# Seven GpSimd operations in the first up step, and two output weight tiles in other places, in a one-core decoder layer

## The chip, the core and the metric

The kernel runs on one core of a Trainium2 chip. The metric is the device time of one execution in microseconds (us). PE is TensorE, DVE is VectorE, ACT is ScalarE, POOL is GpSimd, and SP issues the transfers of this kernel.

## What is computed

One decoder layer on x (1024 rows of 1024, float32). The part that the change touches is the end of the output projection and the start of the MLP:

```python
mixed = concat(out_a, out_b)            # two attention head groups
x  = x + einsum('bse,ed->bsd', mixed, w_out)
hn = rmsnorm(x, mlp_norm_g)
hid = square(relu(einsum('bsd,df->bsf', hn, w_up)))     # 1024 -> 4096
x  = x + einsum('bsf,fd->bsd', hid, w_down)
```

## The kernel before

Every large product is made of float32r parts: `split` (L74 to L80) writes the high part of a tensor with a cast (ACT, L77) and the low part with a subtraction (L80, on POOL or DVE). Three products then stand for one: high by high, high by low, low by high. `mm` is L73, so every matmul of the kernel has that line.

**Output projection.** For each of eight row tiles dt of the transposed output, `out_weights(dt, e0)` loads a weight block `wor` (two buffers), and splits it into a tile `wos`: high part by ACT, low part by POOL. It is called 16 times, counted by i. Calls 1 to 8 are the first halves of the sum (`out_first`, run beside the attention units of the last heads; the partial sums go to `part_d`, after ACT copies them as `pc` and POOL adds them to `xt`). Calls 9 and 10 are the second halves of dt = 0 and 4, run beside the last attention units. Calls 11 to 16 are those of dt = 1, 5, 2, 6, 3, 7, behind the units: 24 products each, which are for each of four inputs e four with the high part of the weights and then two with their low part. The tile of call i lies in the place `w0` or `w1`, by `i % 2`, so a cast of call 11 has to wait until PE has done with call 9.

**Between the two.** `out_finish` (L938 to L959) loads the partial sum as h, adds PE's bank (DVE, L940), writes h to `h_d`, and makes the inputs of the MLP: for each of seven Strassen-like combinations n a high part `bh` (ACT) and a low part `bl` (DVE, L930 or L80), of which some are of sums `ts` (DVE, L947, L959). Nearly all of that is DVE's work, in one order.

**Up.** `up(j)` for j = 0 to 15 takes a raw block `wur` (`up_load`, two transfers, L982), makes four sums `wus` of its quarters with DVE (`plus` L1002, `minus` L999), and splits seven weights n = 1, 2, 3, 6, 7, 5, 4 into tiles `wu`: ACT casts, and the low part is DVE's for n = 2, 6, 5 and POOL's for the others. The places of the `wu` tiles rotate over `w0` to `w6`: the first two of j = 0 lie in `w5` and `w6`. The h of dt = 0 to 3 lie in `w2`, those of dt = 4 to 6 in `w3`, so the `wu` tiles there wait until h has been written out.

**What sets the order.** Each engine runs one instruction stream in order. The framework's scheduler fixes the streams when the program is built; a stream doesn't change when something is late on the chip. Down (L1080 and after) follows up and isn't touched.

Of the kernel before, what the change touches and what calls it, by code (L numbers as in the profile page):

```python
# [9 lines left out]
F32R = mybir.dt.float32r  # L10
# [6 lines left out]
P = 128  # L17
# [38 lines left out]
def hybrid_layer(  # L56
# [13 lines left out]
    nc = tc.nc  # L70

    def mm(out, lhsT, rhs, start, stop):
        return nc.tensor.matmul(out, lhsT, rhs, start=start, stop=stop)  # L73

    def split(hi, lo, src, hi_eng, lo_eng):
        if hi_eng is nc.scalar:
            hi_eng.copy(hi, src)  # L77
        else:
            hi_eng.tensor_copy(hi, src)
        lo_eng.tensor_tensor(out=lo, in0=src, in1=hi.bitcast(F32), op=ALU.subtract)  # L80
# [123 lines left out]
    for t in LAST:  # L204
        eng = (nc.vector.tensor_copy, nc.scalar.copy)[t % 2]
# [604 lines left out]
    def slot(tag, name, shape, dt=F32, pool="zl"):  # L810
        return o[pool].tile([P] + shape, dt, tag=tag, name=name, bufs=1)
# [26 lines left out]
    def out_weights(dt, e0):  # L838
        i = nout[0] = nout[0] + 1
        wr = o["zl"].tile([P, 4, P], F32, tag="wor", name="wor", bufs=2)  # L840
        nc.sync.dma_start(wr, w_o[dt][:, e0 : e0 + 4, :])
        w = slot(f"w{i % 2}", "wos", [2, 4, P], F32R)
        split(w[:, 0], w[:, 1], wr, nc.scalar, nc.gpsimd)
        return w[:, 0], w[:, 1]

# [15 lines left out]
    def out_first(dt):  # L861
        xt = slot(f"w{2 + dt % 2}", "xt", [S])
        nc.sync.dma_start(xt, xT[dt * P : (dt + 1) * P, :])
        w = out_weights(dt, 0)
        ps = first_banks()
        with paced():
            out_products(ps, w, range(4))
        t = slot("w4", "pc", [S])
        for c in range(2):
            cs = slice(c * 512, (c + 1) * 512)  # L870
            nc.scalar.copy(t[:, cs], ps[c])
            nc.gpsimd.tensor_tensor(out=xt[:, cs], in0=xt[:, cs], in1=t[:, cs], op=ALU.add)
        nc.sync.dma_start(part_d[dt], xt)
# [15 lines left out]
    for dt in (0, 4):  # L889
        ps = first_banks() if dt == 0 else [  # L890
            pa.tile([P, 512], F32, tag="sc", name=f"po{c}", bufs=2) for c in range(2)
        ]
        ahead_of.append((dt, ps, out_weights(dt, 4)))
# [85 lines left out]
    def up_load(j):  # L979
        raws[j] = slot(f"r{j % 2}", "wur", [2, KT, P])  # L980
        for i in range(2):
            up_loads[j] = nc.sync.dma_start(raws[j][:, i], w_u[j + i * NJ])  # L982

    for dt in (1, 5, 2, 6, 3, 7):
        w = out_weights(dt, 4)
        ps = [bank(f"po{c}") for c in range(2)]
        out_products(ps, w, range(4, 8))
        out_finish(dt, ps)
        if dt in (2, 3):
            with tc.issue_after(part["load"].ins):  # L990
                up_load(dt - 2)
# [6 lines left out]
    def minus(out, a, b, eng=nc.vector):  # L998
        eng.tensor_tensor(out=out, in0=a, in1=b, op=ALU.subtract)  # L999

    def plus(out, a, b, eng=nc.vector):
        eng.tensor_tensor(out=out, in0=a, in1=b, op=ALU.add)  # L1002
# [3 lines left out]
    def w_slot(name, shape, dt=F32):  # L1006
        nw[0] = (nw[0] + 1) % NW
        return slot(f"w{nw[0]}", name, shape, dt)
# [3 lines left out]
    def up(j):  # L1012
        if 0 < j < NJ - 1:
            up_load(j + 1)
        raw = raws.pop(j)
        s = slot(*(("m4", "wus", [4, 4, P]), ("m5", "wus", [4, 4, P], F32, "zr"))[j % 2 == 0])
        a11, a12, a21, a22 = raw[:, 0, :4], raw[:, 0, 4:], raw[:, 1, :4], raw[:, 1, 4:]
        plus(s[:, 0], a21, a22)
        minus(s[:, 1], s[:, 0], a11)
        minus(s[:, 2], a11, a21)  # L1020
        minus(s[:, 3], a12, s[:, 1])
        src = {1: a11, 2: a12, 3: s[:, 3], 4: a22, 5: s[:, 0], 6: s[:, 1], 7: s[:, 2]}
        m = {}
        for n in UP:
            w = w_slot("wu", [2, 4, P], F32R)
            split(w[:, 0], w[:, 1], src[n], nc.scalar, nc.vector if n in (2, 6, 5) else nc.gpsimd)
            m[n] = bank(f"pu{n}")
            for k in range(4):
                mm(m[n], w[:, 0, k], bh[n][:, k], k == 0, False)
                mm(m[n], w[:, 0, k], bl[n][:, k], False, False)  # L1030
                mm(m[n], w[:, 1, k], bh[n][:, k], False, k == 3)
            if n == 2 and j == 0:
                part.pop("rest")()
            if n == 1:
                u = slot("m1", "u", [4, 512])
                b = slot("m2", "hb", [4, 512])
                nc.scalar.copy(u[:, 0], m[1])
            if n == 2:
                plus(b[:, 0], m[2], u[:, 0])
            if n == 6:  # L1040
                plus(u[:, 1], m[6], u[:, 0])
            if n == 7:
                plus(u[:, 2], m[7], u[:, 1])
            if n == 5:
                minus(u[:, 3], u[:, 1], m[5])
                minus(b[:, 2], u[:, 2], m[5])
                plus(b[:, 3], m[3], u[:, 3])
            if n == 4:
                plus(b[:, 1], m[4], u[:, 2])
        return lambda: up_end(j, b)  # L1050

    def up_end(j, b):
        nc.scalar.activation(b, b, AF.Relu)
        nc.scalar.activation(b, b, AF.Square)  # L1054
        t = slot("m3", "ht", [4, 512])
        b11, b21, b22, b12 = (b[:, i] for i in range(4))
        minus(t[:, 0], b11, b12)
        plus(t[:, 1], b22, t[:, 0])
        minus(t[:, 2], b22, b12)
        minus(t[:, 3], b21, t[:, 1])  # L1060
        nc.sync.dma_start(hid_d[0:3, j].rearrange("n p c -> p n c"), b[:, :3])
        nc.sync.dma_start(hid_d[3:7, j].rearrange("n p c -> p n c"), t)
# [187 lines left out]
    for j in range(NJ):  # L1250
        end = up(j)
        if j < NJ - 1:
            end()
        if 1 <= j <= KT:
            square_of(j - 1)
        if j == KT + 1:
            mean_square()
# [67 lines left out]
```

## Time and profile before

| | us |
|---|---|
| median of 3 runs | 1100.29 |
| lowest and highest | 1097.19 and 1101.08 |
| the profiled execution, its own time | 1097.17 |
| its span, first to last instruction | 1095.5 |
| PE busy | 1081.4 |
| DVE busy | 774.7 |
| ACT busy | 571.6 |
| POOL busy | 365.2 |

In the rows below, a row of a timeline begins with the start in us from the span's start and the duration in us (of a merged row: from the first's start to the last's end). What stands in brackets at its end is how long the engine stood idle before it, and what ended that.

### The profile page before, as it was taken

Reading aid. Unit: us, or ns where it says so; the run is one execution under the profiler, and the core shown is the slowest. Engines: PE = TensorE matmul, PEld = TensorE weight load, DVE = VectorE, ACT = ScalarE, POOL = GpSimd, SP = SyncE. Lnnn points to the kernel's source line nnn. Section 1 sums busy time; section 2 is a strip of 40 time slices with the busy share of each in tenths; the row PEclk is TensorE's granted clock in tenths of the full one; section 3 lists DMA queues with packets and bytes.
Section 4 is the critical chain, followed back from the end, with each engine's and each line's share of the span. In section 5 each row is a group of like instructions: output and inputs, shape, how many; then the busy total and the mean of one; then the engine's idle time right before and its main releaser. Section 6 shows DMA issues by size and latency. Waiting matters only on the chain.

```text
span 1095.5 us, 15678 instructions
## 1 busy us (share of the span) xinstructions
PE 1081.4 (99%) x5557; PEld 934.0 (85%) x5557; DVE 774.7 (71%) x1327; ACT 571.6 (52%) x1013; POOL 365.2 (33%) x352
## 2 busy tenths in 40 slices
PE   9999999999998999999999999999999999999998
PEld 8999999999996888778888888888888888888886
DVE  8377677766777883898686869765665867674395
ACT  5558588676767764554545454443633433333331
POOL 5672523435433564223223232332222222222100
PEclk9999999999999999999999999999999999999999
DMA  8401212334347457663554443344898876665423
GB/s 301 146 23 52 71 38 61 115 93 149 116 154 279 156 174 280 228 214 127 195 194 177 172 165 143 144 173 144 311 391 312 306 288 230 233 224 186 174 91 115
DMA packets 96079, 195.69 MB, mean 179 GB/s; under 512 B 7376, under 2 KB 19584, under 8 KB 96000
## 3 DMA queue, kind: packets, MB, share of 16 engines
q1 hardware_dynamic: 95856, 194.66, 50.9%
q8 instruction: 44, 0.72, 0.3%
q14 instruction: 35, 0.29, 0.1%
q10 hardware_dynamic: 144, 0.02, 0.0%
HBM read 141.61 MB, written 53.04 MB: 178 GB/s over the span
## 4 chain that ended last, share of the span: by engine, by line
PE 86%; DVE 6%; DMA 5%; issue 1%; ACT 1%; POOL 1%; SPq 0%; ACTq 0%; DVEq 0%
PE pd L73 27%; PE pu L73 27%; PE ps L73 13%; PE po L73 5%; PE spb L73 3%; PE pvb L73 3%; PE tpb L705 3%; DMA xr<-in_xT_dram 1%; PE sp L73 1%; PE pv L73 1%; DMA xq<-in_x_dram 1%; PE tpa L534 1%; DMA h_d<-h 1%; PE ptk L302 1%; DVE bl L80 1%
## 5 line engine op out<-in xcount | busy, mean ns | idle before, releaser
L73 PE MATMUL pd<-hx,wx 128*128 128x512 f32 (+1 forms) x1350 | 304.9, 388 | 0.0
L73 PEld LDWEIGHTS pd<-hx,wx 128*128 128x128 f32 x1350 | 252.7, 188 | 52.2
L73 PE MATMUL pu<-bh,wu 128*128 128x512 f32 x896 | 276.5, 390 | 1.1 <-ACT wu L77 1.1
L73 PEld LDWEIGHTS pu<-bh,wu 128*128 128x128 f32 x896 | 168.2, 188 | 36.6 <-ACT wu L77 1.6
L73 PE MATMUL ps<-w,xh 128*128 128x384 f32 (+1 forms) x640 | 176.0, 345 | 0.7 <-DVE z L431 0.6
L73 PE MATMUL pu<-bl,wu 128*128 128x512 f32 x448 | 174.5, 390 | 0.6 <-DVE bl L80 0.6
L77 ACT CAST hx<-hr 128x1024 fp32r<-128x1024 f32 x56 | 58.9, 1052 | 176.6 <-PE pd L73 170.6
L80 POOL TENSOR_TENSOR wx<-wda,wx 128x1024 fp32r<-128x1024 f32 x24 | 64.5, 2686 | 196.4 <-ACT wx L77 169.1
L80 DVE TENSOR_TENSOR hx<-hr,hx 128x1024 fp32r<-128x1024 f32 x56 | 72.3, 1299 | 72.4 <-ACT hx L77 72.4
L73 PEld LDWEIGHTS ps<-w,xh 128*128 128x128 f32 x640 | 115.3, 189 | 3.1 <-DVE z L431 1.0
L73 PE MATMUL ps<-w,xl 128*128 128x384 f32 (+1 forms) x320 | 109.8, 344 | 0.0
L73 PEld LDWEIGHTS pu<-bl,wu 128*128 128x128 f32 x448 | 84.1, 188 | 19.2 <-DVE bl L80 1.0
L73 PE MATMUL po<-mix,wos 128*128 128x512 f32 x384 | 94.0, 395 | 1.0 <-ACT wos L77 0.7
L80 POOL TENSOR_TENSOR wu<-wus,wu 128x512 fp32r<-128x512 f32 x32 | 47.2, 1476 | 127.2 <-ACT wu L77 127.2
L73 PEld LDWEIGHTS po<-mix,wos 128*128 128x128 f32 x384 | 70.4, 188 | 15.5 <-ACT wos L77 1.1
L80 POOL TENSOR_TENSOR wu<-wur,wu 128x512 fp32r<-128x512 f32 x32 | 43.3, 1354 | 88.7 <-ACT wu L77 88.7
L77 ACT CAST wu<-wus 128x512 fp32r<-128x512 f32 x64 | 38.4, 618 | 58.8 <-PE pu L73 55.1
L374 DVE TENSOR_TENSOR ptl<-tpb,pth 128x512 fp32r<-128x512 f32 (+1 forms) x80 | 49.3, 631 | 25.1 <-ACT pth L373 23.1
L999 DVE TENSOR_TENSOR ht<-hb 128x512 f32<-128x512 f32 x32 | 21.8, 722 | 63.2 <-ACT hb L1054 63.2
L80 POOL TENSOR_TENSOR w<-wr,w 128x384 fp32r<-128x384 f32 (+1 forms) x47 | 51.5, 1106 | 41.2 <-ACT w L77 29.3
L77 ACT CAST wx<-wda 128x1024 fp32r<-128x1024 f32 x56 | 58.2, 1044 | 6.7 <-DMA wda<-in_w_d_dram 6.6
L73 PEld LDWEIGHTS ps<-w,xl 128*128 128x128 f32 x320 | 60.3, 188 | 1.0
(214 smaller groups left out, 1935.9 us busy)
## 6 DMA issues: line engine op xcount, KB each, us to landing
wda<-in_w_d_dram SPq DMA_DIRECT2D x34, 1024.0 KB, 9.0
hr<-hid_d SPq DMA_DIRECT2D x56, 512.0 KB, 6.0
wur<-in_w_u_dram SPq DMA_DIRECT2D x32, 512.0 KB, 4.3
hid_d<-ht SPq DMA_DIRECT2D x16, 1024.0 KB, 4.3
hid_d<-hb SPq DMA_DIRECT2D x16, 768.0 KB, 3.6
mix<-mixs_d SPq DMA_DIRECT2D x7, 1024.0 KB, 7.4
wr<-in_w_b_dram SPq DMA_DIRECT2D x32, 192.0 KB, 2.5
xr<-in_xT_dram SPq DMA_DIRECT2D x16, 256.0 KB, 4.8
```

The lines of the kernel that those rows point to most:

```text
L73: return nc.tensor.matmul(out, lhsT, rhs, start=start, stop=stop)
L77: hi_eng.copy(hi, src)
L80: lo_eng.tensor_tensor(out=lo, in0=src, in1=hi.bitcast(F32), op=ALU.subtract)
L302: nc.tensor.transpose(pt[:w, j * P : (j + 1) * P], x[:, 4 * c + j, col : col + w], ident)
L374: nc.vector.tensor_tensor(out=lo[:, cols], in0=pt[:, cols], in1=hi[:, cols].bitcast(F32), op=ALU.subtract)
L534: nc.tensor.transpose(tp[:, hh * P : (hh + 1) * P], pts[hh // 2][:, hh % 2, c0 : c0 + P], ident)
L705: nc.tensor.transpose(tp[:, c0 : c0 + P], probs[qi][:, kb * P : (kb + 1) * P], ident)
L999: eng.tensor_tensor(out=out, in0=a, in1=b, op=ALU.subtract)
```

## The change

Two edits. In `out_weights` the tiles of calls 11 and 12 (dt = 1 and 5) move from `w1` and `w0` to `w6` and `w5`. In `up`, for j = 0 alone, the four sums and the low parts of n = 2, 6 and 5 are POOL's and no longer DVE's; with these POOL makes all seven low parts of j = 0.

```diff
-        w = slot(f"w{i % 2}", "wos", [2, 4, P], F32R)
+        w = slot(f"w{i % 2 + (5 if i in (11, 12) else 0)}", "wos", [2, 4, P], F32R)
...
-        plus(s[:, 0], a21, a22)
-        minus(s[:, 1], s[:, 0], a11)
-        minus(s[:, 2], a11, a21)
-        minus(s[:, 3], a12, s[:, 1])
+        eng = nc.vector if j else nc.gpsimd
+        plus(s[:, 0], a21, a22, eng)
+        minus(s[:, 1], s[:, 0], a11, eng)
+        minus(s[:, 2], a11, a21, eng)
+        minus(s[:, 3], a12, s[:, 1], eng)
...
-            split(w[:, 0], w[:, 1], src[n], nc.scalar, nc.vector if n in (2, 6, 5) else nc.gpsimd)
+            split(w[:, 0], w[:, 1], src[n], nc.scalar, nc.vector if j and n in (2, 6, 5) else nc.gpsimd)
```

ACT's stream beside the last attention units. wos_5775 is the tile of call 11 (dt = 1), wos_5601 that of call 10; pc are the copies of the last first half, pth the high parts of transposed probabilities. Before:

```order
L77 CAST mix7_4258<-mtb_5495 64x256
L871 COPY pc_5436<-po0_5410 128x512
L871 COPY pc_5436<-po1_5411 128x512
L77 CAST wos_5601<-wor_5599 128x512
L373 CAST pth_5573<-tpb_5569 128x384
```

and with the change:

```order
L77 CAST mix7_4258<-mtb_5495 64x256
L77 CAST wos_5775<-wor_5773 128x512
L872 COPY pc_5436<-po0_5410 128x512
L872 COPY pc_5436<-po1_5411 128x512
L77 CAST wos_5601<-wor_5599 128x512
L373 CAST pth_5573<-tpb_5569 128x384
```

The cast of call 11 stood behind all attention units and now stands ahead of the copies pc.

POOL's stream from the output weights of dt = 2 (wos_5868) on. wos_5913 is dt = 6, wos_5964 dt = 3, wos_6009 dt = 7; wur_5908 and wus_6053 are the raw block and the sums of up step j = 0; its wu tiles are 6058 (n = 1), 6077 (2), 6098 (3), 6114 (6), 6131 (7), 6148 (5), 6167 (4). Before:

```order
L80 TENSOR_TENSOR wos_5868<-wor_5866,wos_5868 128x512
L80 TENSOR_TENSOR wos_5913<-wor_5911,wos_5913 128x512
L80 TENSOR_TENSOR wu_6058<-wur_5908,wu_6058 128x512
L80 TENSOR_TENSOR wos_5964<-wor_5962,wos_5964 128x512
L80 TENSOR_TENSOR wos_6009<-wor_6007,wos_6009 128x512
L80 TENSOR_TENSOR wu_6098<-wus_6053,wu_6098 128x512
L80 TENSOR_TENSOR wu_6131<-wus_6053,wu_6131 128x512
```

and with the change:

```order
L80 TENSOR_TENSOR wos_5913<-wor_5911,wos_5913 128x512
L80 TENSOR_TENSOR wu_6058<-wur_5908,wu_6058 128x512
L80 TENSOR_TENSOR wu_6077<-wur_5908,wu_6077 128x512
L1003 TENSOR_TENSOR wus_6053<-wur_5908 128x512
L1000 TENSOR_TENSOR wus_6053<-wur_5908 128x512
L80 TENSOR_TENSOR wos_5964<-wor_5962,wos_5964 128x512
L1000 TENSOR_TENSOR wus_6053<-wus_6053,wur_5908 128x512
L80 TENSOR_TENSOR wos_6009<-wor_6007,wos_6009 128x512
L1000 TENSOR_TENSOR wus_6053<-wur_5908,wus_6053 128x512
L80 TENSOR_TENSOR wu_6114<-wus_6053,wu_6114 128x512
L80 TENSOR_TENSOR wu_6148<-wus_6053,wu_6148 128x512
```

One operation on the raw block stood ahead of the low part of dt = 3, and now four stand there.

PE's stream at the start of dt = 3, which reads the same before and after:

```order
L73 MATMUL po0_5967<-mix4_5442,wos_5964 128x512 [waits DVE_49,Activation_49]
L73 MATMUL po0_5967<-mix4_5442,wos_5964 128x512
L73 MATMUL po1_5968<-mix4_5442,wos_5964 128x512 [waits DVE_49]
L73 MATMUL po1_5968<-mix4_5442,wos_5964 128x512
L73 MATMUL po0_5967<-mix4_5442,wos_5964 128x512 [waits Pool_49]
L73 MATMUL po1_5968<-mix4_5442,wos_5964 128x512
```

Its fifth product is the first that takes the low part, behind four with the high part.

## Rows read from the trace of the kernel before

**Rows 1.** The page's busy times.

```profile
PE 1081.4 (99%) x5557; PEld 934.0 (85%) x5557; DVE 774.7 (71%) x1327; ACT 571.6 (52%) x1013; POOL 365.2 (33%) x352
```

**Rows 2.** Busy time of each engine by stretch: up from its second step on.

```profile
536.00:760.00 224.00, 224.00 (x986) 184.79 (x985) 164.73 (x230) 104.89 (x131) 66.81 (x48) 1.00 0.46 170
```

**Rows 3.** The waits of PE from 425 to 540 us, all of them: total, times, longest.

```profile
PE pu L73 <- ACT wu L77: 1.1, 1, 1.1
PE po L73 <- ACT wos L77: 0.7, 1, 0.7
PE pu L73 <- DVE bl L80: 0.6, 1, 0.6
PE po L73 <- DMA mix<-mixs_d: 0.3, 1, 0.3
PE pvb L73 <- DVE mtb L722: 0.3, 1, 0.3
```

**Rows 4.** PE's timeline: beside the last units, and from dt = 1 to up.

```profile
427.84 0.35 PE L73 MATMUL pvb<-pth,vb 128*128 128x256 f32 x1
428.54 1.66 PE L73 MATMUL po<-mix,wos 128*128 128x512 f32 x6 [0.35 <-DMA mix<-mixs_d]
...
444.11 32.93 PE L73 MATMUL po<-mix,wos 128*128 128x512 f32 x144 [0.69 <-ACT wos L77]
476.88 0.39 PE L73 MATMUL pu<-bh,wu 128*128 128x512 f32 x1
```

**Rows 5.** ACT's timeline: beside the last units, at call 11, at the first up block.

```profile
425.65 1.08 ACT L871 COPY pc<-po 128x512 f32<-128x512 f32 x2 [2.09 <-PE po L73]
...
427.28 1.34 ACT L373 CAST pth<-tpb 128x384 fp32r<-128x384 f32 x3
...
443.45 1.12 ACT L77 CAST wos<-wor 128x512 fp32r<-128x512 f32 x2
...
462.51 1.14 ACT L77 CAST wu<-wur 128x512 fp32r<-128x512 f32 x2 [2.02 <-DMA wur<-in_w_u_dram]
```

**Rows 6.** SP's timeline: the weights of call 11, and the load of h ahead of the up block.

```profile
422.29 0.33 SPq L841 DMA_DIRECT2D wor<-in_w_o_dram  x1
...
457.11 0.32 SPq L938 DMA_DIRECT2D h<-part_d  x1
```

**Rows 7.** Issue to landing (last number, us) of the weights issued at 422.29.

```profile
wor<-in_w_o_dram SPq DMA_DIRECT2D x1, 256.0 KB, 3.6
```

**Rows 8.** The chain that ended last, two of its transfers: start, duration.

```profile
457.48 5.01 DMA wur<-in_w_u_dram
...
473.07 7.55 DMA h_d<-h
```

**Rows 9.** Issue to landing of the third up block, issued at 488.64.

```profile
wur<-in_w_u_dram SPq DMA_DIRECT2D x2, 512.0 KB, 3.9
```

**Rows 10.** POOL's timeline around dt = 3, and in the second up step.

```profile
463.21 1.30 POOL L80 TENSOR_TENSOR wu<-wur,wu 128x512 fp32r<-128x512 f32 x1 [4.86 <-ACT wu L77]
464.77 1.45 POOL L80 TENSOR_TENSOR wos<-wor,wos 128x512 fp32r<-128x512 f32 x1 [0.26 <-ACT wos L77]
467.70 1.42 POOL L80 TENSOR_TENSOR wos<-wor,wos 128x512 fp32r<-128x512 f32 x1 [1.49 <-ACT wos L77]
...
497.81 3.96 POOL L80 TENSOR_TENSOR wu<-wus,wu 128x512 fp32r<-128x512 f32 x2 [6.91 <-ACT wu L77]
```

**Rows 11.** DVE's timeline beside and behind those POOL operations.

```profile
463.69 1.37 DVE L80 TENSOR_TENSOR wu<-wur,wu 128x512 fp32r<-128x512 f32 x1
...
467.29 0.68 DVE L80 TENSOR_TENSOR bl<-ts,bh 128x512 fp32r<-128x512 f32 x1
467.89 1.78 DVE L930 SCALAR_TENSOR_TENSOR bl<-h,vt,bh 128x512 fp32r<-128x512 f32 x1
...
470.19 0.74 DVE L947 SCALAR_TENSOR_TENSOR ts<-h,vt,b 128x512 f32<-128x512 f32 x1
```

**Rows 12.** The instructions on the tiles wu: duration in ns, min/median/max.

```profile
L80 POOL TENSOR_TENSOR wu<-wus,wu x32: 1290/1452/2266, 482.5 to 762.4; 128x512 fp32r<-128x512 f32 x32
```

## The prediction

> **What bounds the kernel now.** I read the page first, then the stretch behind the change, then PE's waits, then the streams of the engines that PE waits for. PE is busy for 1081.4 of the span's 1095.5 us [rows 1], and from 536 us on it has no idle time: 224.00 of 224.00 us [rows 2]. Whatever is gained or lost can therefore only be idle time of PE ahead of that, and it moves the end one for one. PE's waits from 425 to 540 us are five [rows 3]: 0.3 for the load of a mix tile and 0.3 for DVE beside the last units; 0.7 for ACT's cast of call 11 (dt = 1), which stands at 444.11 [rows 4]; 1.1 for a cast and 0.6 for a low part at the start of up. They sum to 3.0 us, and the last three, which the change is about, to 2.4. About 0.5% (5.5 us) is what a measurement of this kernel can tell from no change; so even with every wait of the stretch gone the change could not be told from none. The question is what it adds.
>
> **The change part by part.**
>
> *Places of calls 11 and 12.* Before, the cast of call 11 sits behind the units, at 443.45 [rows 5], because `w1` is PE's until then, and PE waits for it. In `w6` it needs no such wait, so the 0.7 goes: -0.7. But the cast now stands ahead of the copies pc on ACT. Its weights are issued at 422.29 and take 3.6 [rows 6, 7], so they are there at 425.9; the copies began at 425.65 [rows 5]. With one cast of about 0.6 (two in 1.12, rows 5 at 443.45) the copies begin at 426.5, some 0.85 late, and so does the first high part pth behind them: 427.28 becomes 428.1, done at 428.6 (three take 1.34). PE's product on it, which began at 427.84 [rows 4], moves to 428.6. PE stood idle after it anyway until 428.54, so only what lies past that counts: the next product starts 0.12 to 0.35 later (a product's pitch or its full 0.35), at 428.7 to 428.95 in place of 428.54. I take +0.3; the ends are 0 and +0.85.
>
> On POOL the low part of call 11 also moves ahead, one operation of about 1.3, before the zero fills of the last units; PE reaches those fills later than the product above and I cost it at nothing; without that cover it would be at most its 1.3. On SP the weight loads of calls 12 to 16 are issued earlier, since their buffers come free earlier. They are the same transfers; nothing in rows 3 waits for one, and if they slow a neighbour it is the mix load, whose wait is 0.3 now. I cost them at nothing too. Up's first two wu tiles now share `w5` and `w6` with dt = 5 and 1, of which PE is done long before 462.51, when ACT casts them [rows 5]: no cost.
>
> *Sums and low parts on POOL.* DVE loses seven operations of 0.68 [rows 11]: 4.8 us. POOL gets seven. What they cost there: the nearest rows are 1.30, 1.45 and 1.42 [rows 10], mean 1.39. The place matters more than the number. POOL's stream puts the low part of n = 2 and two sums ahead of the low part of dt = 3. Before, one operation stood there (463.21), and the low part of dt = 3 followed at 464.77 [rows 10]. Now five operations end with it: 6058, 6077, two sums, 5964. The up block sets their start: its load is issued at 457.48 and takes 5.01 [rows 8], ACT casts at 462.51 and POOL starts 0.7 later, at 463.2. I leave that start where it is, since the h load that precedes it (457.11, rows 6) follows work of DVE that the change leaves alone. Then 5964 is done at 463.2 + 5 x 1.39 = 470.15.
>
> When does PE ask for it? It starts dt = 1 at 444.11 - 0.69 + 0.3 = 443.7. Products come every (476.88 - 444.11) / 144 = 0.2276 us [rows 4]. dt = 1, 5, 2 and 6 are 96 of them, 21.85 us, so dt = 3 begins at 465.6, and its fifth product, the first with the low part, is due at 466.5. PE then stands for 470.15 - 466.5 = 3.65 us, with nothing to do in its place, since its stream is fixed. This is the new wait: **+3.65**. Bounds: with a load as quick as the third block's, 3.9 [rows 9], and POOL at 1.30, it is 462.1 + 6.5 - 466.5 = 2.1; with POOL at 1.98 each (two in 3.96, rows 10) it is 463.2 + 9.9 - 466.5 = 6.6. dt = 7 comes 24 products after dt = 3; on POOL there are two operations more for it, 2.8 us against 5.5, so no second wait.
>
> *The two waits in up.* With the new wait PE reaches up at 476.88 - 0.69 + 0.3 + 3.65 = 480.1, some 3.3 late. The 1.1 hung on a cast that stood behind the write of h, 473.07 + 7.55 = 480.6 [rows 8]; that write belongs to dt = 6, ahead of the new wait, and doesn't move with it. PE is now later than the cast: -1.1. The 0.6 hung on the last low parts of DVE, which ran without a pause to there. I don't count on the 4.8 us taken off it. Beside POOL's operations DVE's take longer: 1.37 for one of 0.68, 1.78 for one of 0.74 [rows 11], that is 0.7 to 1.0 per POOL operation, so seven more give back 4.8 to 7.3 us. But DVE also waits for PE at dt = 3, and that pause of 3.65 lets it catch up: -0.6.
>
> The Trainium skill (SBUF — State Buffer, "Who interferes with whom") says that a DVE instruction with two SBUF inputs and a GpSimd instruction that reads SBUF exclude each other, the second waiting until the first is done. Rows 10 and 11 agree: both stretched DVE rows lie beside a POOL operation. By that rule alone DVE would not be relieved, and my sum stands as it is, since it takes nothing for the relief.
>
> *Sum.* +0.3 - 0.7 + 3.65 - 1.1 - 0.6 = +1.55 us. The profiled execution took 1097.17, so that is 1098.7 for one like it; it lies 3.1 under the median of the runs, 1100.29, and with the sum on the median the forecast is **1101.8**. Its own ends: the new wait at 2.1 gives 1100.3, at 6.6 it gives 1104.8.
>
> **The rivals.**
>
> *No new wait.* If POOL were through by 466.5, the sum would be +0.3 - 2.4 = -2.1, or 1098.2. For it: POOL has pauses of 4.86, 0.26 and 1.49 us ahead of its three operations there [rows 10]. Against it: five operations would have to run in 3.3 us, 0.66 each where none is under 1.29 [rows 12], or the block would have to land after 1.4 where the quickest takes 3.9 [rows 9]. A mix of both is 1 in 10.
>
> *POOL kept out by DVE: slower.* The place is the same, ahead of dt = 3. POOL's operations of this form take up to 2.27 [rows 12]. DVE's are back to back here; if each POOL operation finds one in its way at that price, 5964 is done at 463.2 + 11.3 = 474.5 and PE waits 8.0: +0.3 - 2.4 + 8.0 = +5.9, or 1106.2. It is slower by over 0.5% from 2.2 per operation on (a wait of 7.6). For it: the pair at 1.98. Against it: the three rows right there are 1.30 to 1.45, with DVE busy. 1 in 10. This is what the rule of the skill's SBUF page would do if DVE always came first.
>
> *Relief that does not relieve.* The new wait comes, but the 1.1 and 0.6 stay: POOL, with seven low parts of j = 0 in one line, is late with the weights of up, or DVE, slowed by it, is late with the last low parts. Then the sum is +1.55 + 1.7 = +3.25, or 1103.5. For it: rows 11. Against it: PE comes 3.3 us later to that place. 15 in 100.
>
> **How the numbers follow.** Forecast 0.62, relief that fails 0.15, no new wait 0.10, POOL kept out 0.10, anything else 0.03. The range, 1097.0 to 1105.5, takes in the forecast's ends, the no-wait case less the scatter of the runs, and the failed relief; it leaves out the upper half of POOL kept out. Over 0.5% faster would need more than all of PE's waits of the stretch, 3.0: 0.02. Slower by over 0.5%: about half of POOL kept out and a little of the rest, 0.06. Within: 0.92.
>
> **What would show it.** Right: PE's wait for `wos` on ACT at 444 is gone; a wait of PE for POOL's `wos` of 2 to 6.6 us stands near 466; the waits in up are gone; POOL runs from 463 to past 473 with hardly a pause; DVE has pauses behind 466. Wrong: no wait for POOL at dt = 3, or one at up in its place; copies pc that still begin at 425.65; or idle time of PE behind 536.

## The result and the profile after

The changed kernel takes 1103.93 us (median of 10 runs, 1101.63 to 1106.58), the kernel before, timed beside it, 1099.89 (10 runs, 1097.19 to 1102.61). The ratio is 1.0035, with a 95% interval from 1.0022 to 1.0048: slower by 0.35%, some 4 us, less than the 0.5% that counts as a difference here, but more than the +1.55 us of the sum: even the low end of the interval is +2.4 us. The time lies in the range. The profiled execution took 1103.9 us (span 1102.2).

The page's busy times, which answer to [rows 1]:

```profile
PE 1084.1 (98%) x5557; PEld 937.1 (85%) x5557; DVE 767.2 (70%) x1320; ACT 575.1 (52%) x1013; POOL 378.1 (34%) x359
```

Seven instructions went from DVE to POOL. DVE lost 7.5 us, POOL gained 12.9, or 1.84 for each. PE executes the same 5557 matmuls, yet is busy for 2.7 us more: some of them ran longer.

PE's waits from 425 to 540 us (in total, times, longest), which answer to [rows 3]:

```profile
PE po L73 <- POOL wos L80: 4.4, 1, 4.4
PE po L73 <- DMA mix<-mixs_d: 1.1, 1, 1.1
PE pvb L73 <- ACT pth L373: 1.0, 1, 1.0
PE pvb L73 <- DVE mtb L722: 0.3, 1, 0.3
```

The three waits that the change was about, 0.7, 1.1 and 0.6, are gone. In their place stands one of 4.4 for POOL, and two of about 1 beside the last units. PE's timeline, which answers to [rows 4]; the number in brackets is the idle time before the row:

```profile
428.89 0.39 PE L73 MATMUL pvb<-pth,vb 128*128 128x256 f32 x1 [0.98 <-ACT pth L373]
430.34 2.57 PE L73 MATMUL po<-mix,wos 128*128 128x512 f32 x6 [1.06 <-DMA mix<-mixs_d]
...
441.21 28.47 PE L73 MATMUL po<-mix,wos 128*128 128x512 f32 x124
474.07 7.85 PE L73 MATMUL po<-mix,wos 128*128 128x512 f32 x24 [4.40 <-POOL wos L80]
```

Six products took 2.57 us behind the first pauses (1.66 before), and 24 took 7.85 behind the long one, where 24 at 0.2276, with the 0.16 by which the last one's row outlasts its pitch, are 5.62. The granted clock tells why. Busy time by stretch of the kernel after (span, its length, then PE, PEld, DVE, ACT and POOL busy with their counts, granted clock, DMA share, GB/s):

```profile
430.00:435.00 5.00, 4.66 (x18) 4.08 (x19) 0.49 (x1) 0.37 (x1) 2.48 (x6) 0.66 1.02 416
432.00:433.00 1.00, 1.00 (x5) 0.81 (x4) 0.00 (x0) 0.00 (x0) 0.47 (x3) 0.50 1.05 430
...
472.00:479.00 7.00, 4.93 (x12) 3.89 (x13) 6.96 (x6) 2.96 (x5) 6.63 (x5) 0.53 0.72 248
```

Behind the two short pauses and in and behind the long one the clock stood at its lower level, 1.2 GHz, for some microseconds: a granted clock of 0.50 from 430.8 to 434.2 and from 471.7 to 478.6 (0.66 and 0.53 are means over stretches that it did not fill). From 435 to 471 and from 479 to 540 it is 1.00. In the kernel before, the same two stretches have 1.00:

```profile
430.00:435.00 5.00, 4.65 (x27) 3.77 (x26) 2.22 (x5) 2.21 (x5) 1.02 (x5) 1.00 1.01 361
...
472.00:479.00 7.00, 7.00 (x33) 5.79 (x32) 7.00 (x13) 4.00 (x7) 0.00 (x0) 1.00 0.85 274
```

This is not the profile's alone. Of every timed execution the mean granted clock is on record: it averages 0.995 over the ten of the kernel after and 0.998 over 94 of the kernel before (those timed beside e1 to e11 below). A difference of 0.003 over 1100 us is 3.3 us of clock, an estimate of the most that it can cost, since a lower clock during a pause costs nothing. The scatter of the kernel before goes with it too: its executions at 0.996 took 1101.8 on average, those at 0.999 and 1.000 took 1098.2.

POOL's timeline after, which answers to [rows 10]:

```profile
465.93 3.07 POOL L80 TENSOR_TENSOR wu<-wur,wu 128x512 fp32r<-128x512 f32 x2 [15.30 <-ACT wu L77]
468.96 1.71 POOL L1003 TENSOR_TENSOR wus<-wur 128x512 f32<-128x512 f32 x1
470.64 1.71 POOL L1000 TENSOR_TENSOR wus<-wur 128x512 f32<-128x512 f32 x1
472.31 1.71 POOL L80 TENSOR_TENSOR wos<-wor,wos 128x512 fp32r<-128x512 f32 x1
473.98 1.28 POOL L1000 TENSOR_TENSOR wus<-wus,wur 128x512 f32<-128x512 f32 x1
475.22 1.73 POOL L80 TENSOR_TENSOR wos<-wor,wos 128x512 fp32r<-128x512 f32 x1
```

The first five operations (the first row holds two) stand in the order that the prediction gave, and the low part of dt = 3 is the fifth. It ends at 474.02, and PE restarts at 474.07. They took 8.09 us, or 1.62 each.

### The profile page after: what moved, and what is told of

Read it like the earlier page. It is cut to its first block, busy times and chain, and to the rows that moved or that the text cites. A ratio compares the mean times of both kernels' runs of the same rounds, so it can differ in the third digit from the quotient of the medians.

```text
span 1102.2 us, 15681 instructions
## 1 busy us (share of the span) xinstructions
PE 1084.1 (98%) x5557; PEld 937.1 (85%) x5557; DVE 767.2 (70%) x1320; ACT 575.1 (52%) x1013; POOL 378.1 (34%) x359
## 4 chain that ended last, share of the span: by engine, by line
PE 88%; DVE 5%; DMA 4%; POOL 1%; issue 1%; ACT 1%; SPq 0%; ACTq 0%; DVEq 0%
PE pu L73 28%; PE pd L73 27%; PE ps L73 13%; PE po L73 6%; PE spb L73 4%; PE pvb L73 3%; PE tpb L705 3%; DMA xr<-in_xT_dram 1%; PE sp L73 1%; PE pv L73 1%; DMA xq<-in_x_dram 1%; PE tpa L534 1%; DMA mix<-mixs_d 1%; PE ptk L302 1%; DVE k2z L346 0%
## 5 line engine op out<-in xcount | busy, mean ns | idle before, releaser
L73 PE MATMUL po<-mix,wos 128*128 128x512 f32 x384 | 97.3, 405 | 5.5 <-POOL wos L80 4.4
L80 POOL TENSOR_TENSOR wu<-wus,wu 128x512 fp32r<-128x512 f32 x34 | 51.3, 1509 | 122.0 <-ACT wu L77 122.0
```

## The experiments

The theory from these rows: (A) the loss is call 15's low part (dt = 3) standing fifth in POOL's queue, with the clock that falls behind the pause; (B) the rival: the two places cost something too, by the cast of call 11 ahead of ACT's copies. A third (C): POOL's work beside DVE's is dear wherever it stands. In the text, "up" is the sum of PE's waits for pu's operands at the first up block; waits of PE under 0.35 us are left out of the rows from here on. The ratios are against the kernel before, timed beside e1 to e4, beside e5 to e8, and beside e9 to e11.

**e1_places: the places alone.** The kernel before, with this one line:

```diff
-        w = slot(f"w{i % 2}", "wos", [2, 4, P], F32R)
+        w = slot(f"w{i % 2 + (5 if i in (11, 12) else 0)}", "wos", [2, 4, P], F32R)
```

> The two output weight places alone, without the GpSimd part. Theory (the loss beside the last units is the cast of call 11 ahead of ACT's queue and the mix load behind it, plus half-clock matmuls after those two pauses): PE's 0.7 us wait at the start of dt = 1 is gone, but two waits of about 1 us each appear beside the units, granted clock 0.5 for some us behind them; the waits 1.1 and 0.6 in up stay; no wait for POOL at dt = 3. Together +1 to +2.5 us against before. Rival (the late loads in the one profile were scatter): waits beside the units as before, 0.3 and 0.3, and -0.7 us.

Measured: 1102.55 us, ratio 1.0024 (1.0010 to 1.0037). PE's waits:

```profile
PE pu L73 <- DVE bl L930: 1.6, 2, 1.2
PE pu L73 <- ACT wu L77: 1.6, 1, 1.6
PE pvb L73 <- ACT pth L373: 1.4, 1, 1.4
PE po L73 <- DMA mix<-mixs_d: 0.7, 1, 0.7
PE pu L73 <- DVE bl L80: 0.6, 1, 0.6
PE pu L73 <- ACT bh L929: 0.4, 1, 0.4
```

The places alone are slower. The 0.7 is gone, but up waits 4.2 us where it waited 1.7 [rows 3] (expected: no change there), and PE waits 1.4 for pth. The expected fall of the clock came too: 0.50 from 433.1 to 436.5, behind the pauses of 1.4 and 0.7. Seven transposes there take 1.70 us, which take 0.93 in e5 below:

```profile
433.52 1.70 PE L705 MATMUL tpb<-ident,sb 128*128 128x128 f32 x7
```

**e2_pool: POOL's part alone.** The other lines of the change, with calls 11 and 12 in their old places.

> The GpSimd part alone, places as before. Theory (POOL's queue): the 0.7 us wait at dt = 1 stays; at dt = 3 PE waits 3 to 4.5 us for POOL's low part and works at clock 0.5 behind it, some 2 us more; the waits in up are gone (-1.7): +3.5 to +5 us. Rival (the loss is DVE, held up at the port by POOL): a short wait at dt = 3 or none, and low parts of DVE (bl) late in up, 2 us or more.

Measured: 1103.79 us, ratio 1.0042 (1.0027 to 1.0057).

```profile
PE po L73 <- POOL wos L80: 4.0, 1, 4.0
PE po L73 <- DMA mix<-mixs_d: 2.1, 1, 2.1
PE po L73 <- ACT wos L77: 0.7, 1, 0.7
```

The 24 products behind the pause again ran long (7.34 us), with a granted clock of 0.84 from 471 to 482. The wait, the clock and the time are as A expected. So POOL's part alone makes about all of the whole change's loss. The two parts do not add: 1.0024 and 1.0042 against 1.0035. In the profiles this is because the places lose in up, and where PE comes late by 4 us it finds up's operands ready.

**e3_order: the whole change, POOL's sums and its low parts from n = 2 on behind call 15's low part.**

```diff
+        behind = lambda: nullcontext() if j else tc.issue_after(lows[15].ins)
+        with behind():
             plus(s[:, 0], a21, a22, eng)
...
+            with behind() if n != 1 else nullcontext():
                 split(w[:, 0], w[:, 1], src[n], nc.scalar, nc.vector if j and n in (2, 6, 5) else nc.gpsimd)
```

> The whole change, with the sums and the other low parts of j = 0 tied on POOL behind the low part of call 15 (dt = 3); as many POOL operations as with the change. Theory (POOL's queue): no wait of PE for POOL at dt = 3, clock 1.0 from 440 us on; the loss beside the units stays: 5 to 7 us less than the change in a profile, 3 to 5 in the medians, so -0.5 to +1.5 us against before. Rival (DVE held up by the seven extra POOL operations): as slow as the change, +4 us, with waits on DVE in up.

Measured: 1101.45 us, ratio 1.0021 (1.0009 to 1.0034).

```profile
PE pu L73 <- DVE bl L932: 1.9, 3, 0.7
PE pvb L73 <- ACT pth L373: 1.4, 1, 1.4
PE po L73 <- POOL wos L80: 1.1, 1, 1.1
PE pu L73 <- ACT bh L931: 0.4, 1, 0.4
```

With one tie the wait for POOL falls from 4.4 to 1.1 (now for call 16, dt = 7), and the clock stays at 1.00 from 428 to 484. A is confirmed for what it says of the wait and the clock. The times alone do not show the gain, since this interval and that of the whole change overlap; the pair e2 and e6 below does. And a loss of 0.2% remains, some 2.3 us where A expected at most 1.5: up waits 2.3 us, as PE now comes early enough to meet up's late operands again.

**e4_hold: the places, with call 11's cast kept behind the copy of the last unit but one.** The edit against e1:

```diff
+        with tc.issue_after(mtbs[-2].ins) if i == 11 else nullcontext():
-        split(w[:, 0], w[:, 1], wr, nc.scalar, nc.gpsimd)
+            split(w[:, 0], w[:, 1], wr, nc.scalar, nc.gpsimd)
```

> The places alone as in e1, but call 11's cast on ACT tied behind the copy of the last but one unit, so that it no longer stands ahead of the copies pc. Theory: the wait on ACT beside the units and the 0.7 us at dt = 1 are both gone, clock 1.0 there: -0.7 us against before, 1.5 to 3 less than e1. Rival (scatter): the same as e1.

Measured: 1102.3 us, ratio 1.0028 (1.0014 to 1.0042). The expected -0.7 us was missed; the loss is 3. The wait for pth is gone, and with it the lower clock beside the units (1.00 there), but one of 2.2 for the mix load stands in its place, and up waits 3.7. So the cast ahead of ACT's copies does make PE wait for pth, but to remove it gains nothing here: PE waits for the mix load instead.

**e5_before: the kernel before, unchanged, profiled again.** Is the late mix load the change's?

> The kernel before, unchanged, profiled beside the other experiments. If the pause for the mix load and the stretch at 320 to 340 us are scatter, its profile may have either: a wait of PE for the mix load between 0 and 2.2 us, a clock between 0.94 and 1.00 at 320 to 340. In any case no wait of PE for ACT's pth over 0.3, a wait of 0.7 for ACT's wos at dt=1 and 1.0 to 2.5 in up. If, against that, late mix loads belong to the places or to GpSimd's part, its wait is below 0.5 and the clock 1.00. Ratio 0.999 to 1.001 either way.

Measured: 1099.42 us, ratio 0.9996 (0.9985 to 1.0007); span 1097.3.

```profile
PE po L73 <- DMA mix<-mixs_d: 2.3, 1, 2.3
PE pu L73 <- ACT wu L77: 0.9, 1, 0.9
PE po L73 <- ACT wos L77: 0.7, 1, 0.7
PE pu L73 <- DVE bl L80: 0.5, 1, 0.5
```

and two rows of PE's timeline, the products on the mix tile and the start of dt = 1:

```profile
430.56 1.65 PE L73 MATMUL po<-mix,wos 128*128 128x512 f32 x6 [2.25 <-DMA mix<-mixs_d]
446.15 32.95 PE L73 MATMUL po<-mix,wos 128*128 128x512 f32 x144 [0.69 <-ACT wos L77]
```

It is not the change's. The kernel before pauses there for 0.3 us in one profile and for 2.3 in another, which accounts for the difference between their spans, 1095.5 and 1097.3. The profile that the prediction rests on has the short pause. Where the mix load is late, PE's products on it begin at 430.56 here, and at 430.34 in the kernel after, which ran 0.2 ahead of this profile before the units: its wait of 1.0 for pth cost nothing beside a late mix load. Over all profiles the waits for pth and mix together are 1.2 to 2.1 us with the cast first (the change, e1, e3, e8), 0.3 to 2.3 without the places (before, e2, e5, e6, e9) and 1.0 to 2.2 with the cast held (e4, e7, e10, e11): what the cast costs there is lost in what the mix load scatters.

**e6_pool_order: POOL's part alone, with e3's tie.**

> GpSimd's part without the two places, and the sums and low parts after n=1 tied behind call 15's low part. If the place in GpSimd's queue is what GpSimd's part costs (4.0 us of wait and a lower clock behind it), PE waits for GpSimd's wos at most 1.1 us, the clock is 1.00 from 470 to 480, the wait of 0.7 for ACT's wos stays and the time is that of before within 1.5 us: ratio 0.999 to 1.0015. If GpSimd's work itself is dear wherever it stands (slower VectorE beside it, sums that come late), up waits 4 us or more and the ratio is 1.003 or above.

Measured: 1102.02 us, ratio 1.0018 (1.0007 to 1.0029). PE waits 0.9 for POOL, 0.7 for ACT's wos, and 2.7 in up where e5 waits 1.4; the clock is 1.00. The expectation of A, 0.999 to 1.0015, was missed, and that of C, 1.003 or more, too: the order is worth over half of what POOL's part costs, not all of it (0.0024 of 0.0042; worked out from the two intervals, 0.0005 to 0.0043). What is left goes with C: up is not relieved. How DVE's instructions stand beside POOL's is seen in the kernel after, DVE's timeline (to be read with POOL's rows above):

```profile
469.47 1.75 DVE L948 SCALAR_TENSOR_TENSOR ts<-h,vt,b 128x512 f32<-128x512 f32 x1
...
474.13 1.68 DVE L960 SCALAR_TENSOR_TENSOR ts<-h,vt,ts 128x512 f32<-128x512 f32 x1
475.73 1.76 DVE L960 SCALAR_TENSOR_TENSOR ts<-h,vt,b 128x512 f32<-128x512 f32 x1
...
479.77 0.74 DVE L960 SCALAR_TENSOR_TENSOR ts<-h,vt,ts 128x512 f32<-128x512 f32 x1
```

The same form takes 0.74 alone and 1.68 to 1.76 beside POOL. POOL's takes 1.28 where it began first (473.98, DVE's 474.13 beside it ends 0.55 after it) and 1.71 to 1.73 where DVE's began first (475.22, which ends 1.14 after DVE's 474.13 does). By these rows the two engines take turns, and a pair costs each of them some 1.7 us. An addition that reads PE's bank (h<-po,h) is not stretched: two took 1.28 beside POOL (472.82). From 462 to 500 us the kernel before runs 51 DVE instructions, 8 of them stretched, by 6.7 us in all; after it is 45, 10 of them stretched, by 9.0 (what a row takes beyond 0.60 for each instruction and 0.08 once, counted from 0.3 on). Six instructions fewer spare 3.6 us, and 2.3 of that are given back (an estimate from two profiles; against e5, with 6.2, it is 2.8).

**e7_hold_order: the whole change with both ties, e3's and e4's.**

> The whole change with both ties: call 11's cast behind the copy of the last unit but one, GpSimd's sums behind call 15's low part. If both causes add, PE waits neither for ACT's pth nor more than 1.1 us for GpSimd's wos, and of the 4 us some 3 are gone: ratio 0.999 to 1.0015. If the pause for pth only hid the pause for the mix load behind it, the first tie gives nothing beyond the second, and the ratio is that of the whole change with the second tie alone, 1.001 to 1.0034.

Measured: 1100.29 us, ratio 1.0015 (1.0003 to 1.0027). PE's waits: 1.5 for mix, 1.0 for POOL, 2.5 in up, none for pth. Both expectations hold this ratio; their intervals overlap, so this run does not tell them apart. By the ratios, over half of the loss of the whole change is its order (0.0020 of 0.0035; the two intervals just overlap).

**e8_low15_dve: the whole change, call 15's low part on DVE.**

```diff
-        split(w[:, 0], w[:, 1], wr, nc.scalar, nc.gpsimd)
+        split(w[:, 0], w[:, 1], wr, nc.scalar, nc.vector if i == 15 else nc.gpsimd)
```

> The whole change, with call 15's low part on VectorE. If the wait of 4.4 us is GpSimd's queue, it is gone, with the half clock behind it, and what is left is the price of the two places: ratio 1.001 to 1.003, as with the tie. If VectorE is as late with it, PE waits for VectorE's wos, 1 us or more, and the clock falls again; if the sums hold up the units instead, up waits 2 us or more for wu. Then the ratio stays at 1.003 to 1.005.

Measured: 1101.86 us, ratio 1.0021 (1.0011 to 1.0031). The wait at dt = 3 is gone, as A has it, and the clock is 1.00 throughout; but POOL's four sums now run ahead of call 16's low part, and PE waits 1.7 for that at dt = 7, and 2.4 in up. It ends where e3 does, by another way to the same repair. The mean granted clock over the timed executions agrees with the profiles: 0.995 and 0.996 with the wait at dt = 3 (the change, e2), 0.998 to 0.999 where it is repaired (e3, e6, e7, e8), 0.998 before.

**e9_late_sums: the kernel before, with three of the four sums on POOL, behind call 16's low part.** There POOL stood idle for 13.4 us.

```diff
-        minus(s[:, 1], s[:, 0], a11)
-        minus(s[:, 2], a11, a21)
-        minus(s[:, 3], a12, s[:, 1])
+        eng = nc.vector if j else nc.gpsimd
+        with nullcontext() if j else tc.issue_after(lows[16].ins):
+            minus(s[:, 1], s[:, 0], a11, eng)
+            minus(s[:, 2], a11, a21, eng)
+            minus(s[:, 3], a12, s[:, 1], eng)
```

> The kernel before, with the three sums after the first on GpSimd and behind call 16's low part, where it stood idle for 13.4 us; no low part moves, no place changes. If VectorE's backlog alone holds up, its three instructions of 0.6 us fewer cut the 1.4 to 1.7 us that PE waits in up to 0.5 or less: ratio 0.998 to 1.000. If VectorE loses beside GpSimd's instructions what it is spared (some 1 us on each instruction that is stretched), up still waits 1.4 to 3 us: ratio 1.000 to 1.0015. No wait for GpSimd's wos and a clock of 1.00 from 440 to 500 by both.

Measured: 1099.91 us, ratio 1.0010 (0.9995 to 1.0024): no difference shown. Up waits 2.1 us (1.4 in e5), and the clock, which was expected at 1.00, is 0.50 from 492.9 to 496.3, behind the waits of 0.6 to 0.8 in up. DVE runs 48 instructions from 462 to 500, 9 of them stretched by 7.7. This is POOL's part at its best place, in nobody's way, and DVE gains nothing by it: what it is spared (three of 0.60, 1.8 us) it mostly loses beside POOL's (stretched by 1.0 us more than in the first profile of before, and by 1.5 more than in e5, where 51 instructions are stretched by 6.2).

**e10_dve_order: e4, with DVE's sums and n = 2's low part tied behind the additions of dt = 2, where they stood before.** Why does up wait longer with the places?

```diff
+        with nullcontext() if j else tc.issue_after(part[2, 1].ins):
+            plus(s[:, 0], a21, a22)
...
+            with tc.issue_after(part[2, 0].ins) if j == 0 and n == 2 else nullcontext():
```

> The two places with call 11's cast held, and VectorE's low part of n=2 and its sums tied behind the additions of dt=2, as they stood before. If the 3.7 us that PE waits in up with the places alone come from VectorE's changed order, they fall to 2.1 or less (1.4 of before and the 0.7 gained at dt=1 given back): ratio 0.999 to 1.001. If they come from somewhere else (the products' own order in up, ScalarE's casts, the store of h that call wu's slot waits for), up stays at 3 to 4 us and the ratio at 1.002 to 1.004.

Measured: 1100.54 us, ratio 1.0014 (1.0002 to 1.0026). Up waits 3.4 us, not 2.1 or less, while the ratio lies between the two that were expected. So the reading that it is DVE's order is not borne out. It is not settled either, since the tie took hold of one sum and what hangs on it, but not of the third sum, which waits for the block ahead of dt = 2's additions (DVE's timeline of e10; before, no sum stands there):

```profile
468.63 0.69 DVE L1001 TENSOR_TENSOR wus<-wur 128x512 f32<-128x512 f32 x1 [1.74 <-DMA wur<-in_w_u_dram]
469.24 0.69 DVE L942 TENSOR_TENSOR h<-po,h 128x512 f32<-128x512 f32 x1
```

PE's timeline of e10, the rows in up that have a wait:

```profile
485.88 0.50 PE L73 MATMUL pu<-bl,wu 128*128 128x512 f32 x1 [0.43 <-DVE bl L932]
487.82 0.50 PE L73 MATMUL pu<-bh,wu 128*128 128x512 f32 x1 [1.21 <-ACT wu L77]
495.66 0.50 PE L73 MATMUL pu<-bl,wu 128*128 128x512 f32 x1 [1.19 <-DVE bl L932]
497.96 0.50 PE L73 MATMUL pu<-bl,wu 128*128 128x512 f32 x1 [0.65 <-DVE bl L80]
```

The second of these hangs on a write: ACT's cast for n = 6 takes the place of a tile that is being written to memory (dt = 6's h). ACT's row in e5 and in e4:

```profile
482.51 0.62 ACT L77 CAST wu<-wus 128x512 fp32r<-128x512 f32 x1 [2.26 <-DMA h_d<-h]
```

```profile
485.10 1.14 ACT L77 CAST wu<-wus 128x512 fp32r<-128x512 f32 x2 [2.77 <-DMA h_d<-h]
```

(In e10 the row, at 486.01, names the load of rr, but that lands at 487.1; the write, issued at 477.25, landed at 486.0.) SP's timeline of e5,

```profile
475.01 0.36 SPq L941 DMA_DIRECT2D h_d<-h  x1
475.42 0.74 SPq L938 DMA_DIRECT2D rr<-part_d  x1
```

and of e4:

```profile
475.33 0.43 SPq L940 DMA_DIRECT2D rr<-part_d  x1
475.87 5.98 SPq L943 DMA_DIRECT2D h_d<-h  x2
```

With the places SP issues the load of rr ahead of that write. The write takes 7.4 us from issue to landing in e5, 9.2 in e4, and 8.7 in e10, where it goes first again; so its place on SP is at most 0.5 of the 1.8, and the rest is not explained. The two waits for L932, 1.6 in all, are the same in e4 and e10, and new against e5; the order of the products in up differs there from before, and no run tried that by itself.

**e11_hold_late: e4 with e9's sums,** the combination that could have beaten both kernels.

> The two places with call 11's cast held, and the three sums on GpSimd behind call 16's low part. If what the places gain is lost to VectorE's backlog in up, relief of VectorE at a time that is in nobody's way keeps it: up waits below 2 us, no wait for GpSimd's wos, ratio 0.997 to 0.9995, faster than both kernels. If relief does not reach up, it waits 3 to 4 us as with the places alone: ratio 1.002 to 1.004.

Measured: 1101.68 us, ratio 1.0025 (1.0014 to 1.0037). No wait for POOL, but up waits 3.9 us (2.4 of it for ACT's bh), and the clock is 0.50 from 482.8 to 486.2. It is not faster. No version here beats the kernel before.

## Why the prediction was right, and where its sum was off

The class and the range were right, and so was the main mechanism, the new wait at dt = 3; the sum came out at less than half of the 4 us, and what it lacked is the clock. By its steps, with e5 as the profile of before (span 1097.3 against 1102.2, +4.9):

- *-0.7 for call 11's wait:* right, the row is gone.
- *+0.3 beside the last units:* the cast does stand ahead of pc and pth, and PE does wait for it (1.0). A late mix load covers it, as the start of the products on mix shows (430.34 against 430.56 in e5); that the mix load was late in the profile after is luck for this step. What the step lacked is the clock: behind the two pauses of about 1 us it stood at 0.50 for 3.4 us, and there six products took 2.57 for 1.65 and seven transposes 1.56 for 0.93, +1.55. dt = 1 begins at 446.67 (441.21 + 24 x 0.2276; 24 of that row's 124 products are still of dt = 0 and 4) against 446.15 in e5: +0.5 net, although it holds the -0.7.
- *+3.65 for POOL's low part at dt = 3:* right in place and cause, too small. The gap from POOL's start to PE's demand was forecast at 3.3 us and is 3.5 (465.93 to 469.43); the price of an operation was taken as 1.39 and was 1.62. Five of them make 8.1 in place of 6.95. From demand to the low part's end that is 4.6; the row's 4.40 counts from the end of the last product. The mis-sized term is the 1.39: the rows it came from [rows 10] each had a pause of POOL ahead; behind one another they take 1.71 where DVE's two-input instructions run beside them.
- *Missing: the clock behind that pause.* 24 products take 7.85 in place of 5.62, +2.2. This is the step that failed: the prediction had that whatever is gained or lost can only be idle time of PE, and so priced a pause at its own length, with nothing for the work behind it. That it hangs on the long pause is shown by e3, e6 and e8: with 0.9 to 1.7 in its place the clock is 1.00 there. That it is no matter of one profile is shown by the mean clock of the executions.
- *-1.1 and -0.6 in up:* right, both are gone, because PE comes late. In e5 they are 0.9 and 0.5, but PE regains more than the listed waits: the second product of up and the one 75 products later are 19.42 us apart in e5 and 17.00 in the kernel after (rows below), -2.4. The rest is in longer rows, which no list of waits counts (two products at 490.57 in e5 take 0.96 us, where two take 0.61 elsewhere).
- *Sum with these sizes:* +0.5 + 4.6 + 2.2 - 2.4 = +4.9, which is the profiles' 4.9. The medians differ by 4.0 (2.4 to 5.3 by the interval).

The two products of up, in e5:

```profile
479.17 0.39 PE L73 MATMUL pu<-bl,wu 128*128 128x512 f32 x1
...
498.59 0.39 PE L73 MATMUL pu<-bl,wu 128*128 128x512 f32 x1
```

and in the kernel after:

```profile
486.52 0.39 PE L73 MATMUL pu<-bl,wu 128*128 128x512 f32 x1
...
503.52 0.39 PE L73 MATMUL pu<-bl,wu 128*128 128x512 f32 x1
```

The rivals: *no new wait* fell at once. *POOL kept out by DVE* came true in part, since 1.62 lies between the forecast's 1.39 and its 2.27. *Relief that does not relieve* did not show in the whole change, where PE's late coming hides up. Where the new wait is cut short (e3, e6, e8), up waits 2.3 to 2.7 us again: in these runs the relief of DVE does not pay even without the new wait. The rule that the prediction weighed (the Trainium skill, SBUF — State Buffer, "Who interferes with whom": a VectorE instruction with two SBUF inputs contends with a GpSimd instruction that reads SBUF) agrees with the rows: 0.74 against 1.7 on DVE, 1.28 against 1.71 on POOL, as the one or the other began first.

The prediction also set its profile 3.1 us under the median and carried the sum over to the median. That was right: e5 shows that some 1.9 us of it is the mix load (2.25 against 0.35), and the mean clock of that profile, 0.999, is above the average of 0.998.

Open: the rest of why up waits longer with the places (e10), what makes the mix load late in one profile and not in another, and the same of the clock. The profiles of e1 to e4, e6 and e7 show a granted clock of 0.94 to 0.96 from 320 to 340 us, and that of e10 0.50 from 339.9 on, where the profiles of before and after have 1.00; it lies ahead of the instructions that these edits move, and no run tied it to one of them. The mean clock of the kernel before, 0.996 to 1.000 from one execution to the next, says that such falls happen in it too. So single profiles of two kernels can differ by some 2 us for no reason of theirs, and the account above, of one profile each, has that uncertainty.

## What to carry to other kernels

An operation that goes to an idle engine is priced by what stands behind it in that engine's queue: here 6.4 us of work, most of it of no hurry, stood ahead of one low part that PE needed in 3.5. Look for the first instruction in the queue that the bottleneck waits for, and tie the newcomers behind it (e6: a ratio of 1.0018 in place of e2's 1.0042). When a pause of PE is forecast, add the products behind it that may run at the lower clock. And where two engines stretch each other, count what comes back before counting the relief: of 3.6 us spared, some 2.3 came back.

## What was not expected of the hardware

The clock's answer to a pause is not a matter of its length alone. After 4.40 us of pause (and 4.00 in e2) the products behind it ran at the lower level; after 2.25 us in e5 the stretch from 430 to 435 kept 1.00, and after two pauses of 0.98 and 1.06 in the kernel after it fell to a mean of 0.66 there, with PE busy for 4.66 of the 5.00 us. e1, the other profile with two such pauses there (1.4 and 0.7), fell as well; the others, with one pause there of 0.3 to 2.3, did not. In e9 and e11, with waits of 0.3 to 2.4 us in up, the stretch from 480 to 500 has 0.91; in e8 and e1, with 2.4 and 4.2 us of them in all, it has 1.00. And the lower level stands while PE works again, not only while it is idle: 24 products took 7.85 us. The Trainium skill (TensorE: Matmul & The Clock Gate, "Part 1: The HAM clock gate") says that the full clock is released by activity and withdrawn without it. The rows of the long pause agree, with 0.53; what decides behind the shorter ones no run here shows.
